# Seven block products instead of eight in some down-projection units of the first layer

## The chip, the cores and the metric

The program runs on one core of a Trainium2 chip. The metric is the device time of one execution in microseconds. A core has TensorE (PE, matmuls, with its weight loads PEld), VectorE (DVE), ScalarE (ACT), GpSimd (POOL) and SyncE (SP), which here issues the weight loads; the ACT queue issues the other DMAs. Each engine has a queue of its own and takes its instructions in order.

## The reference

A decoder trunk of two layers on 256 tokens, width 2048, all in float32: a gated-linear-attention layer, then a forgetting-attention layer, each followed by a channel mixer. What the change touches is the channel mixer:

```python
def conv_ffn(h, w_up, conv_w, conv_b, w_down):
    u = causal_dwconv(h @ w_up, conv_w, conv_b)
    a, val = split_cols(u, [FFN_HIDDEN, FFN_HIDDEN])
    return (jax.nn.silu(a) * val) @ w_down
...
        h = rmsnorm(x, norm_ffn[i])
        x = x + conv_ffn(h, ffn_w_up[i], ffn_conv_w[i], ffn_conv_b[i], ffn_w_down[i])
```

FFN_HIDDEN is 5632, so `w_down` is 5632 x 2048. The change is in the product with `w_down`, in the first layer alone.

## The kernel before

**Products.** A float32 product is made of three fast matmuls: every operand is split into a high half (rounded by a cast) and a low half (the rest), and the kernel adds high x high, low x high and high x low. Tokens are the stationary operand (blocks of 128 tokens, `b` = 0 and 1, from the lists A and B, which hold both halves of every 128-row chunk), weights are the moving one (128 x 512).

**Units and panels.** The weights lie packed in the order of use. A unit is two chunks of 128 rows by 512 columns, 128 x 1024 in SBUF. A panel is the 512 output columns of one projection over all its chunks; its two PSUM accumulators `acc` are for the two token blocks. For each unit SP loads `raw` (4 buffers), ACT casts it to `whi` (L206, 3 buffers), DVE subtracts for `wlo` (L215, 3 buffers), and PE does 2 chunks x 2 blocks x 3 = 12 matmuls: first the eight that read `whi` (L227, L228), then the four that read `wlo` (L231). `split_unit` gives the load, the cast and the subtraction a higher priority, so that they run ahead of PE as far as buffers allow.

**The channel mixer** (`ffn`) takes the hidden chunks in three parts: 16, 16 and 12. In each part the up panels come first. An up panel's output is scaled on ACT (L896), transposed on DVE (L298), written to DRAM (`turned`, L301) and read back as `u` (four reads, L306); then `taken` does the convolution (L881 on ACT, L882 and L883 on DVE), the gate (L885, L886) and the split into A (L378, L379), for two chunks. These steps are set by `later` a number of units after the panel, so those of the last up panel run while PE is in the down-projection.

**The down-projection** (`add_out`) has four panels, f = 0 to 3, of 8 units each (6 in the last part). Panels 0 and 1 go through `proj_two`: all but the last unit of panel 0, then of panel 1, then the last units; panels 2 and 3 go through `proj_tm` one after the other. At the end of a panel DVE adds the two accumulators into the residual `x` (L854). PSUM has four `acc` banks and four work banks (tags t, s, s, o).

**What sets the order.** A scheduler orders each engine's queue when the program is built, from the order and the priority in the code; `passed` counts units and starts the steps that `later` has set.

Of the kernel before, what the change touches and what calls it, by code (L numbers as in the profile page):

```python
# [135 lines left out]
def _trunk(ctx: ExitStack, tc: tile.TileContext, xt, xtok, memt, wp, wgu, gns, gfin, cnv, par, msk, out):  # L136
    nc = tc.nc
    where, _ = _layout()
    V, S, TE = nc.vector, nc.scalar, nc.tensor

    const = ctx.enter_context(tc.tile_pool(name="const", bufs=1))
    wpool = ctx.enter_context(tc.tile_pool(name="wpool", bufs=4))
# [3 lines left out]
    pacc = ctx.enter_context(tc.tile_pool(name="pacc", bufs=4, space=PSUM))  # L146
# [16 lines left out]
    x = [const.tile([P, 2, 512], F32, name=f"x{f}") for f in range(4)]  # L163
# [3 lines left out]

    with tc.high_priority(offset=2 * AHEAD):
        V.memset(bufB[KC - 1].bitcast(F32), 0.0)
# [4 lines left out]
    loads, casts, due = [], [], []  # L174

    def later(*steps):

        for units, step in steps:
            due.append([units, step])

    def passed():

        for d in due:
            d[0] -= 1
        for d in [d for d in due if d[0] == 0]:
            due.remove(d)
            with tc.issue_after(casts[-1].ins):
                d[1]()
# [3 lines left out]
    def work(tag, bufs=1):  # L192
        return pwork.tile([P, 512], F32, name="ps_" + tag, tag=tag, bufs=bufs)

    def load_unit(unit, pieces=1, before=None, pool=wpool):
        off, kcs, n = unit
        w = len(kcs) * n
        raw = wpool.tile([P, NUNIT], F32, name="raw", tag="raw", bufs=4)
        hi = pool.tile([P, NUNIT], F32R, name="whi", tag="whi", bufs=3)
        src = wp[off : off + P * w].rearrange("(p n) -> p n", p=P)  # L200
        for i in range(pieces):
            if before is not None:
                before(i)
            s = slice(i * w // pieces, (i + 1) * w // pieces)
            loads.append(nc.sync.dma_start(raw[:, s], src[:, s]))
            casts.append(S.activation(hi[:, s], raw[:, s], AF.Copy))  # L206
        return raw, hi, w

    def split_unit(unit, pieces=1, before=None, pool=wpool):
        with tc.high_priority(offset=AHEAD):  # L210
            raw, hi, w = load_unit(unit, pieces, before, pool)
            lo = pool.tile([P, NUNIT], F32R, name="wlo", tag="wlo", bufs=3)
            for i in range(pieces):
                s = slice(i * w // pieces, (i + 1) * w // pieces)
                V.tensor_tensor(lo[:, s], raw[:, s], hi[:, s].bitcast(F32), ALU.subtract)  # L215
        passed()
        return hi, lo
# [34 lines left out]
    def proj_two(keys, src, evacs, late):  # L252

        units = [where[k] for k in keys]
        base = min(min(u[1]) for u in units[0])
        acc = [[pacc.tile([P, 512], F32, name="acc", tag="acc") for _ in range(2)] for _ in keys]
        count = len(units[0])
        for part in (range(count - late), range(count - late, count)):
            for i in range(2):
                for u in part:  # L260
                    unit = units[i][u]
                    hi, lo = split_unit(unit)
                    products(list(enumerate(acc[i])), src, base, unit, hi, lo, u == 0, u == count - 1)
                if part[-1] == count - 1:
                    for b in range(2):
                        evacs[i](b, acc[i][b][:, : units[i][0][2]])

    def turned(pool, bank, width, col):

# [102 lines left out]
    def split(dst, i, src, g=None, dealt=True):  # L372

        hi, lo = dst[i][:, 0, :], dst[i][:, 1, :]
        if dealt:
            hi, lo, src = halved(hi), halved(lo), natural(src)
        if g is None:
            S.activation(hi, src, AF.Copy)  # L378
            V.tensor_tensor(lo, src, hi.bitcast(F32), ALU.subtract)  # L379
# [127 lines left out]
    with tc.tile_pool(name="load", bufs=1) as lp:  # L507
# [36 lines left out]
        sq, acc = [x[f].rearrange("p b (c t) -> p (b c) t", t=T) for f in range(2)]  # L544
# [303 lines left out]
            add_out(("wo", 1), mix, then, late=2)  # L848


    def add_out(key, src, then=None, spare=None, late=1):
        def evac(f):
            def out(b, a):
                V.tensor_tensor(x[f][:, b, :], x[f][:, b, :], a, ALU.add)  # L854
                if then is not None:
                    then(f, b)

            return out

        proj_two([(*key, f) for f in range(2)], src, [evac(f) for f in range(2)], late)  # L860
        for f in range(2, 4):
            proj_tm((*key, f), src, evac(f), spare if f == 3 else None)

    def ffn(l, nx, h, m, then, spare=None):
        with tc.tile_pool(name=f"ffn{l}", bufs=1) as fp:
            cw = fp.tile([P, 4 * 88], F32, name="cw")
            nc.sync.dma_start(cw, cnv[l])
            us = [fp.tile([P, 4, T + 2], F32, name=f"u{i}") for i in range(2)]
            for u in us:
                nc.gpsimd.memset(u[:, :, :2], 0.0)  # L870
            turn = [0]

            def taken(j, base, u, i):

                cv = []
                for c in range(2):
                    v = u[:, 2 * c + i, :]
                    col = (c * 44 + j + i) * 4
                    w = [cw[:, col + n : col + n + 1] for n in range(4)]
                    r = fp.tile([P, T], F32, name=f"cv{c}", tag=f"cv{c}", bufs=3)  # L880
                    S.activation(r, v[:, 2:], AF.Identity, bias=w[3], scale=w[2])  # L881
                    V.scalar_tensor_tensor(r, v[:, 1 : T + 1], w[1], r, ALU.mult, ALU.add)  # L882
                    V.scalar_tensor_tensor(r, v[:, :T], w[0], r, ALU.mult, ALU.add)  # L883
                    cv.append(r)
                S.activation(cv[0], cv[0], AF.Silu)  # L885
                V.tensor_tensor(cv[1], cv[0], cv[1], ALU.mult)  # L886
                split(m, j + i - base, cv[1])

            def panel(j, base, slack=0):
                held = []  # L890

                def evac(b, a):
                    if not held:
                        held.append(Turn("turned"))
                    e = tp.tile([P, 512], F32, name="scaled", tag="scaled", bufs=2)
                    S.activation(e, a, AF.Copy, scale=nx.col()[:, b : b + 1])  # L896
                    held[0].put(b, e)
                    if not b:
                        return
                    u = us[turn[0] % 2]  # L900
                    turn[0] += 1
                    later((3, held[0].write), (6, lambda: held[0].read(lambda k: u[:, k, 2:])),
                          (8 + slack, lambda: taken(j, base, u, 0)), (9 + slack, lambda: taken(j, base, u, 1)))

                return evac

            for p, (lo, hi) in enumerate(PARTS):
                js = list(range(lo, hi, 2))
                if not p:
                    proj_two([("up", l, j) for j in js[:2]], h, [panel(js[0], lo), panel(js[1], lo, 2)], 2)  # L910
                    js = js[2:]
                for j in js:
                    proj_tm(("up", l, j), h, panel(j, lo))
                end = p == len(PARTS) - 1
                add_out(("down", l, p), m, then if end else None, spare if end else None)

    def preparing(name, dst):
        n = StreamNorm()
# [147 lines left out]
```

## Time and profile before

| | |
|---|---|
| median of 3 runs | 2254.09 us (2254.07 to 2255.87) |
| profiled execution | 2254.47 us, span 2252.7 us |
| granted TensorE clock | 0.999 |
| PE busy | 2239.9 us, 10336 matmuls |
| DVE, ACT busy | 1525.7 us, 1276.5 us |
| weight loads | 427 MB on SP's queue |

Rows of the timeline read: start and length in microseconds, engine (with q: its queue issues a DMA), line, operation, tiles written <- tiles read, shapes, how many follow each other, and in brackets the idle time before and what ended it. Lines are those of the kernel before. In the profiled execution the down-projection of the first layer begins near 643.9 us (part 0), 905.1 (part 1) and 1122.6 (part 2).

### The profile page before, as it was taken

The numbers are of one execution on the slowest core, as the hardware profiler recorded it, in microseconds if no ns is written. First come the engines' busy times: TensorE is split into PE (matmuls) and PEld (weight loads), VectorE is DVE, ScalarE is ACT, GpSimd is POOL, SyncE is SP. The second block draws the span as 40 slices with busy tenths as digits, with TensorE's granted clock in tenths as the row PEclk, the third lists the DMA queues.
The fourth block names the chain that finished last, engine by engine and source line by source line (L and its number), as shares of the span: only waits on it lengthen the run. The fifth ranks groups of instructions, "written<-read, shape, count | busy, mean of one in ns | idle before, by whom it ended". The sixth has DMA issues, their size and how long they took to land.

```text
span 2252.7 us, 29275 instructions
## 1 busy us (share of the span) xinstructions
PE 2239.9 (99%) x10336; PEld 1874.8 (83%) x10336; DVE 1525.7 (68%) x2317; ACT 1276.5 (57%) x1850; POOL 2.9 (0%) x15
## 2 busy tenths in 40 slices
PE   9999999999999999999999999999999999999998
PEld 7888888888888888888888998888888888888886
DVE  7568988667675576646776556766776467664766
ACT  7555666556553565535665655555655456544654
POOL 0000000000000000000000000000000000000000
PEclk9999999999999999999999999999999999999999
DMA  9875666677775777657777876677776677766774
GB/s 318 279 233 188 207 204 220 205 233 246 250 234 195 227 237 246 209 195 247 234 250 255 257 266 202 181 251 238 244 251 216 196 240 240 242 203 210 239 242 150
DMA packets 303771, 516.96 MB, mean 229 GB/s; under 512 B 178556, under 2 KB 187272, under 8 KB 303496
## 3 DMA queue, kind: packets, MB, share of 16 engines
q1 hardware_dynamic: 124296, 427.24, 57.1%
q10 hardware_dynamic: 179328, 87.85, 13.9%
q8 instruction: 81, 1.33, 0.2%
q14 instruction: 66, 0.54, 0.1%
HBM read 470.44 MB, written 44.58 MB: 229 GB/s over the span
## 4 chain that ended last, share of the span: by engine, by line
PE 98%; DMA 1%; DVE 1%; issue 0%; ACT 0%; SPq 0%; DVEq 0%; ACTq 0%
PE acc L227 32%; PE acc L228 32%; PE acc L231 31%; DMA raw<-wp 0%; PE ps_s L683 0%; PE ps_s L485 0%; PE ps_t L478 0%; PE ps_o L496 0%; DMA xf<-xt 0%; DVE wlo L215 0%; DMA back<-turned 0%; PE ps_s L825 0%; PE ps_o L841 0%; PE ps_o L703 0%; PE ps_s L603 0%
## 5 line engine op out<-in xcount | busy, mean ns | idle before, releaser
L215 DVE TENSOR_TENSOR wlo<-raw,whi 128x1024 fp32r<-128x1024 f32 (+4 forms) x809 | 969.7, 1201 | 636.6 <-ACT whi L206 615.4
L206 ACT ACTIVATE whi<-raw 128x1024 fp32r<-128x1024 f32 (+4 forms) x809 | 842.3, 1043 | 860.0 <-PE acc L228 703.3
L227 PE MATMUL acc<-whi,B 128*128 128x512 f32 (+3 forms) x1792 | 685.7, 384 | 0.0
L228 PE MATMUL acc<-whi,B 128*128 128x512 f32 (+3 forms) x1792 | 684.5, 383 | 0.0
L227 PE MATMUL acc<-whi,A 128*128 128x512 f32 x1440 | 562.3, 392 | 1.4 <-ACT A L378 1.0
L228 PE MATMUL acc<-whi,A 128*128 128x512 f32 x1440 | 559.8, 390 | 0.0
L231 PE MATMUL acc<-wlo,B 128*128 128x512 f32 (+3 forms) x1792 | 469.3, 382 | 0.0
L231 PE MATMUL acc<-wlo,A 128*128 128x512 f32 x1440 | 387.2, 390 | 0.3 <-DVE wlo L215 0.3
L227 PEld LDWEIGHTS acc<-whi,B 128*128 128x128 f32 x1792 | 336.3, 188 | 60.5
L228 PEld LDWEIGHTS acc<-whi,B 128*128 128x128 f32 x1792 | 336.0, 188 | 59.5
L231 PEld LDWEIGHTS acc<-wlo,B 128*128 128x128 f32 x1792 | 333.7, 188 | 59.7
L227 PEld LDWEIGHTS acc<-whi,A 128*128 128x128 f32 x1440 | 270.6, 188 | 60.0 <-ACT whi L206 1.8
L228 PEld LDWEIGHTS acc<-whi,A 128*128 128x128 f32 x1440 | 270.7, 188 | 55.9 <-DVE A L382 0.2
L231 PEld LDWEIGHTS acc<-wlo,A 128*128 128x128 f32 x1440 | 270.0, 188 | 56.6 <-DVE wlo L215 0.7
L881 ACT ACTIVATE cv<-u,cw 128x256 f32<-128x256 f32 x176 | 96.9, 589 | 22.9 <-DMA u<-turned 22.9
L882 DVE SCALAR_TENSOR_TENSOR cv<-u,cw,cv 128x256 f32<-128x256 f32 x176 | 78.2, 479 | 14.9 <-ACT cv L881 14.9
L298 DVE STREAM_TRANSPOSE square<-scaled 128x512 f32<-128x512 f32 x122 | 80.0, 691 | 0.0
L883 DVE SCALAR_TENSOR_TENSOR cv<-u,cw,cv 128x256 f32<-128x256 f32 x176 | 77.1, 479 | 0.0
L854 DVE TENSOR_TENSOR x<-x,acc 128x512 f32<-128x512 f32 x64 | 41.2, 681 | 22.7 <-PE acc L231 22.7
L896 ACT ACTIVATE scaled<-acc,ny 128x512 f32<-128x512 f32 x88 | 54.8, 674 | 0.0
L462 ACT ACTIVATE sq<-x 128x256 f32<-128x256 f32 x80 | 32.5, 408 | 15.4 <-DVE x L854 14.0
L886 DVE TENSOR_TENSOR cv<-cv,cv 128x256 f32<-128x256 f32 x88 | 37.3, 424 | 1.4 <-ACT cv L885 1.4
(179 smaller groups left out, 846.3 us busy)
## 6 DMA issues: line engine op xcount, KB each, us to landing
raw<-wp SPq DMA_DIRECT2D x743, 512.0 KB, 4.2
turned<-square ACTq DMA_DIRECT2D x61, 512.0 KB, 4.5
u<-turned ACTq DMA_DIRECT2D x176, 128.0 KB, 5.2
raw<-wp SPq DMA_DIRECT2D x32, 384.0 KB, 3.1
raw<-wp SPq DMA_DIRECT2D x24, 388.0 KB, 4.5
back<-xturned ACTq DMA_DIRECT2D x64, 128.0 KB, 5.1
xturned<-square ACTq DMA_DIRECT2D x12, 512.0 KB, 4.4
back<-turned ACTq DMA_DIRECT2D x32, 128.0 KB, 4.2
```

Source lines behind the costliest of these rows:

```text
L206: casts.append(S.activation(hi[:, s], raw[:, s], AF.Copy))
L215: V.tensor_tensor(lo[:, s], raw[:, s], hi[:, s].bitcast(F32), ALU.subtract)
L227: TE.matmul(acc[:, :n], xh, hi[:, s], start=first and j == 0, stop=False)
L228: TE.matmul(acc[:, :n], xl, hi[:, s], start=False, stop=False)
L231: TE.matmul(a, xh, ls, start=False, stop=stop)
L298: V.transpose(self.square[:, :, :, b], src.rearrange("p (c t) -> p c t", t=32))
L854: V.tensor_tensor(x[f][:, b, :], x[f][:, b, :], a, ALU.add)
L881: S.activation(r, v[:, 2:], AF.Identity, bias=w[3], scale=w[2])
L882: V.scalar_tensor_tensor(r, v[:, 1 : T + 1], w[1], r, ALU.mult, ALU.add)
L883: V.scalar_tensor_tensor(r, v[:, :T], w[0], r, ALU.mult, ALU.add)
L886: V.tensor_tensor(cv[1], cv[0], cv[1], ALU.mult)
L896: S.activation(e, a, AF.Copy, scale=nx.col()[:, b : b + 1])
```

## The change

In the first layer, the units 1 and 4 of a panel pair are computed together over both panels. Such a seven unit pair is a 2 x 2 x 2 block product (two token blocks, two chunks, two panels). In place of eight block products it forms seven, by Winograd's form of Strassen's method: sums of token blocks (`forms`, made once for each part in `summed`), sums of weight blocks (`t13`, `t24`, on DVE), and sums of the products. Four of the products go to the work banks (`m1`, `m5`, `m6`, `m7`), three straight into `acc`. After the second of the two unit pairs `more` adds the work banks into `x`. `proj_seven` takes the panels of a pair unit by unit, and does so for panels 0, 1 and panels 2, 3 in parts 0 and 1, for panels 0, 1 alone in part 2: five panel pairs. The steps of one seven unit pair are: v0 (both chunks of panel 0's unit, `r0`), v2 (`t13`), v3 (`t24`), and v1 (half of panel 1's unit, `r1`), each with a cast on ACT and a subtraction on DVE, and six (v1: three) matmuls.

```diff
+SEVEN = (1, 4)
...
+    def proj_seven(keys, src, forms, evacs, pool, more):
...
+        acc = [[pacc.tile([P, 512], F32, name="acc", tag="acc") for _ in range(2)] for _ in keys]
+        m1, m5, m6, m7 = (work(t, n) for t, n in (("t", 1), ("s", 2), ("o", 1), ("s", 2)))
...
+        def emit(groups):
+            todo = [g[n] for n in range(2) for g in groups] + [g[2] for g in groups]
...
+        def halves(raw, w, name="w"):
+            hi = wpool.tile([P, NUNIT], F32R, name="whi", tag="whi", bufs=3)
+            casts.append(S.activation(hi[:, :w], raw, AF.Copy))
+            lo = wpool.tile([P, NUNIT], F32R, name="wlo", tag="wlo", bufs=3)
+            V.tensor_tensor(lo[:, :w], raw, hi[:, :w].bitcast(F32), ALU.subtract)
+            return hi, lo
...
+            if u not in forms:
+                for i in range(2):
+                    hi, lo = split_unit(units[i][u])
+                    emit([form(acc[i][b], token(kc, b), hi, lo, c) for b in range(2) for c, kc in enumerate((k0, k1))])
+                    if u == count - 1:
+                        for b in range(2):
+                            evacs[i](b, acc[i][b])
+                continue
+            s = forms[u]
+            with tc.high_priority(offset=AHEAD):
+                r0 = load(units[0][u])
+                v0 = halves(r0, NUNIT)
+                r1 = load(units[1][u])
+            passed()
+            emit([form(m1, token(k0, 0), *v0, 0), form(acc[0][0], token(k1, 0), *v0, 1)])
+            with tc.high_priority(offset=AHEAD):
+                t13 = pool.tile([P, 2, 512], F32, name="t13", tag="t13")
+                V.tensor_tensor(t13[:, 0, :], r1[:, :512], r0[:, :512], ALU.subtract)
+                V.tensor_tensor(t13[:, 1, :], r1[:, 512:], r1[:, :512], ALU.subtract)
+                v2 = halves(t13.rearrange("p c n -> p (c n)"), NUNIT)
+            emit([form(m5, s(0), *v2, 0), form(m7, s(2), *v2, 1)])
+            with tc.high_priority(offset=AHEAD):
+                t24 = pool.tile([P, 2, 512], F32, name="t24", tag="t24")
+                V.tensor_tensor(t24[:, 0, :], r1[:, 512:], t13[:, 0, :], ALU.subtract)
+                V.tensor_tensor(t24[:, 1, :], r0[:, 512:], t24[:, 0, :], ALU.subtract)
+                v3 = halves(t24.rearrange("p c n -> p (c n)"), NUNIT)
+            passed()
+            emit([form(m6, s(1), *v3, 0), form(acc[0][1], token(k1, 1), *v3, 1)])
+            with tc.high_priority(offset=AHEAD):
+                v1 = halves(r1[:, 512:], 512)
+            emit([form(acc[1][0], s(3), *v1, 0)])
+            if u == max(forms):
+                more(m1, m5, m6, m7, pool)
...
+            def more(m1, m5, m6, m7, pool):
+                u = pool.tile([P, 512], F32, name="u", tag="us", bufs=2)
+                w = pool.tile([P, 512], F32, name="w", tag="us", bufs=2)
+                V.tensor_tensor(x0[:, 0, :], x0[:, 0, :], m1, ALU.add)
+                S.activation(u, m1, AF.Copy)
+                V.tensor_tensor(u, u, m6, ALU.add)
+                V.tensor_tensor(x1[:, 0, :], x1[:, 0, :], u, ALU.add)
+                V.tensor_tensor(w, u, m7, ALU.add)
+                V.tensor_tensor(x0[:, 1, :], x0[:, 1, :], w, ALU.add)
+                V.tensor_tensor(x1[:, 1, :], x1[:, 1, :], w, ALU.add)
+                V.tensor_tensor(x1, x1, m5.unsqueeze(1).to_broadcast([P, 2, 512]), ALU.add)
...
+        if forms:
+            seven(0)
+        else:
+            proj_two([(*key, f) for f in range(2)], src, [evac(f) for f in range(2)], late)
+        if forms and then is None:
+            seven(2)
+            return
...
+            def summed(form):
+                h0, h1 = (natural(h) for h in held)
+                held.clear()
+                f = fp.tile([P, 4, P], F32, name="sf", tag="sf")
+                V.tensor_tensor(f[:, 0, :], h0[:, :, 1], h1[:, :, 1], ALU.add)
+                V.tensor_tensor(f[:, 2, :], h0[:, :, 0], h0[:, :, 1], ALU.subtract)
+                V.tensor_tensor(f[:, 1, :], f[:, 0, :], h0[:, :, 0], ALU.subtract)
+                V.tensor_tensor(f[:, 3, :], h1[:, :, 0], f[:, 1, :], ALU.subtract)
+                S.activation(form[:, 0, :, :], f, AF.Copy)
+                V.tensor_tensor(form[:, 1, :, :], f, form[:, 0, :, :].bitcast(F32), ALU.subtract)
```

The order below is of DVE's queue, with the numbers of the buffers. First the place in part 0's first panel pair where the last up panel's convolution steps stand (cv0, cv1, on u1), before:

```order
L215 TENSOR_TENSOR wlo_6197<-raw_6193,whi_6194 128x1024
L882 SCALAR_TENSOR_TENSOR cv0_6199<-u1_4577,cw_4574,cv0_6199 128x256
L882 SCALAR_TENSOR_TENSOR cv1_6203<-u1_4577,cw_4574,cv1_6203 128x256
L883 SCALAR_TENSOR_TENSOR cv0_6199<-u1_4577,cw_4574,cv0_6199 128x256
L883 SCALAR_TENSOR_TENSOR cv1_6203<-u1_4577,cw_4574,cv1_6203 128x256
L215 TENSOR_TENSOR wlo_6227<-raw_6223,whi_6224 128x1024
L882 SCALAR_TENSOR_TENSOR cv0_6229<-u1_4577,cw_4574,cv0_6229 128x256
```

Between these steps only splits of plain units stand. The same place after, from the product of the first chunk to the split of v3 (`raw_6254` is r0 and `raw_6260` r1 of unit pair 4; `wlo_6285` is v2's, `wlo_6298` v3's; L997 and L998 are the L882 and L883 of before, L1001 is L886, L466 is L379):

```order
L1001 TENSOR_TENSOR cv1_6234<-cv0_6230,cv1_6234 128x256
L338 TENSOR_TENSOR t13_6280<-raw_6260,raw_6254 128x512
L339 TENSOR_TENSOR t13_6280<-raw_6260 128x512
L997 SCALAR_TENSOR_TENSOR cv1_6266<-u1_4577,cw_4574,cv1_6266 128x256
L998 SCALAR_TENSOR_TENSOR cv0_6262<-u1_4577,cw_4574,cv0_6262 128x256
L466 TENSOR_TENSOR A14_98<-cv1_6234,A14_98 128x128x2
L344 TENSOR_TENSOR t24_6293<-raw_6260,t13_6280 128x512
L998 SCALAR_TENSOR_TENSOR cv1_6266<-u1_4577,cw_4574,cv1_6266 128x256
L310 TENSOR_TENSOR wlo_6285<-t13_6280,whi_6283 128x1024
L345 TENSOR_TENSOR t24_6293<-raw_6254,t24_6293 128x512
L953 TENSOR_TENSOR x0_80<-x0_80,ps_t_6066 128x512
L1001 TENSOR_TENSOR cv1_6266<-cv0_6262,cv1_6266 128x256
```

The sums and the splits of the second seven unit pair now stand between and behind the convolution steps, and the split of v3 (L310, `wlo_6298`) is the next row. Ahead of these rows stand, in this order, L997 on cv0 and cv1, L998 on cv0, the split of the last plain unit, L998 on cv1, v0's split and L997 on the second cv0.

The second place is the end of part 0's first panel pair, where DVE adds the accumulators into x. Before:

```order
L854 TENSOR_TENSOR x0_80<-x0_80,acc_6046 128x512
L854 TENSOR_TENSOR x0_80<-x0_80,acc_6047 128x512
L215 TENSOR_TENSOR wlo_6407<-raw_6403,whi_6404 128x1024
L854 TENSOR_TENSOR x1_81<-x1_81,acc_6048 128x512
L854 TENSOR_TENSOR x1_81<-x1_81,acc_6049 128x512
```

The two adds of a panel follow each other. After (L941 is L854; `raw_6485` and `raw_6479` belong to unit pair 1 of the next panel pair):

```order
L941 TENSOR_TENSOR x0_80<-x0_80,acc_6062 128x512
L338 TENSOR_TENSOR t13_6493<-raw_6485,raw_6479 128x512
L339 TENSOR_TENSOR t13_6493<-raw_6485 128x512
L216 TENSOR_TENSOR wlo_6465<-raw_6461,whi_6462 128x1024
L941 TENSOR_TENSOR x0_80<-x0_80,acc_6063 128x512
```

Two sums and a split now stand between the adds of panel 0. The third place is the end of part 2's first panel pair, after:

```order
L216 TENSOR_TENSOR wlo_10311<-raw_10307,whi_10308 128x1024
L941 TENSOR_TENSOR x0_80<-x0_80,acc_9973 128x512
L958 TENSOR_TENSOR x0_80<-x0_80,w_10232 128x512
L959 TENSOR_TENSOR x1_81<-x1_81,w_10232 128x512
L216 TENSOR_TENSOR wlo_10329<-raw_10325,whi_10326 128x1024
L385 STREAM_TRANSPOSE square_10264<-x0_80 128x512
L941 TENSOR_TENSOR x0_80<-x0_80,acc_9974 128x512
```

Here two adds of `more`, a split and a transpose stand between the two adds of panel 0.

More of the change, by code (lines that the diff above doesn't have):

```diff
@@ L848, in fox, with add_out @@
             add_out(("wo", 1), mix, then, late=2)
-    def add_out(key, src, then=None, spare=None, late=1):
+    def add_out(key, src, then=None, spare=None, late=1, forms=None, pool=None):
         def evac(f):
@@ L858, in evac, with seven @@
             return out
[L860 removed]
+        def seven(f):
+            x0, x1 = x[f], x[f + 1]
+            def more(m1, m5, m6, m7, pool):
[9 more added lines that the diff above has]
+                V.tensor_tensor(x1, x1, m5.unsqueeze(1).to_broadcast([P, 2, 512]), ALU.add)
+            proj_seven([(*key, g) for g in (f, f + 1)], src, forms, [evac(f), evac(f + 1)], pool, more)
+        if forms:
[5 more added lines that the diff above has]
+            return
         for f in range(2, 4):
@@ L871, in ffn, with form @@
             turn = [0]
+            forms = {u: fp.tile([P, 2, 4, P], F32R, name=f"forms{u}") for u in (SEVEN if spare is None else ())}
+            held = []
+            def form(t):
+                return lambda i: [t[:, h, i, :] for h in range(2)]
             def taken(j, base, u, i):
@@ L914, in ffn @@
                 end = p == len(PARTS) - 1
-                add_out(("down", l, p), m, then if end else None, spare if end else None)
+                add_out(("down", l, p), m, then if end else None, spare if end else None,
+                        forms={u: form(t) for u, t in forms.items()}, pool=fp)
     def preparing(name, dst):
```

36 lines of the change are left out of this document (added).

## The prediction

> **What bounds the kernel now.** I read the page first, for the engines and the chain that ended last.
>
> ```profile
> span 2252.7 us, 29275 instructions
> PE 2239.9 (99%) x10336; PEld 1874.8 (83%) x10336; DVE 1525.7 (68%) x2317; ACT 1276.5 (57%) x1850; POOL 2.9 (0%) x15
> PE 98%; DMA 1%; DVE 1%; issue 0%; ACT 0%; SPq 0%; DVEq 0%; ACTq 0%
> ```
>
> TensorE (PE) is busy 99% of the span and is 98% of the chain. So a matmul that goes is time won, and whatever makes PE wait is time lost, since no later slack takes it back. The change removes matmuls and adds VectorE (DVE) work, so I next read the busy time by stage: both panel pairs of part 0, the first pairs of parts 1 and 2.
>
> ```profile
> 643.90:687.40 43.50, 43.50 (x193) 36.05 (x192) 27.31 (x35) 22.30 (x28) 0.00 (x0) 1.00 0.68 218
> 687.40:730.90 43.50, 43.50 (x193) 36.04 (x192) 21.98 (x21) 16.96 (x17) 0.00 (x0) 1.00 0.57 195
> 905.00:948.50 43.50, 43.50 (x193) 36.04 (x192) 27.31 (x35) 22.31 (x28) 0.00 (x0) 1.00 0.68 218
> 1122.60:1155.30 32.70, 32.70 (x146) 27.07 (x145) 23.01 (x33) 19.68 (x32) 0.31 (x1) 1.00 0.71 230
> ```
>
> The columns are the stretch, then PE, PEld, DVE, ACT and POOL busy (instructions), the granted clock and DMA. PE never pauses; DVE has 27.3 of 43.5 us in a first pair of 16 chunks, 22.0 in a second, 23.0 of 32.7 in part 2: a first pair still holds the convolution of the last up panels. The timeline of PE gives the rhythm, and the waits of part 0's down stage say what ACT and DVE wait for.
>
> ```profile
> 643.90 0.39 PE L227 MATMUL acc<-whi,A 128*128 128x512 f32 x1
> 644.13 0.39 PE L228 MATMUL acc<-whi,A 128*128 128x512 f32 x1
> 645.72 1.07 PE L231 MATMUL acc<-wlo,A 128*128 128x512 f32 x4
> 646.62 0.39 PE L227 MATMUL acc<-whi,A 128*128 128x512 f32 x1
> ACT whi L206 <- PE acc L228: 45.4, 28, 3.0
> DVE wlo L215 <- ACT whi L206: 34.7, 25, 2.3
> ```
>
> A unit of 12 matmuls takes 2.72 us, so 0.227 a matmul. ACT waits only for PE to give a whi buffer back, DVE for ACT: today both run as far ahead as three buffers let them.
>
> **What goes.** Eight block products of three matmuls become seven: 3 x 0.227 = 0.68 us for each seven unit pair. Five panel pairs with two such pairs each make 30 matmuls, **-6.8 us**. The number of loads is the same.
>
> **What is added, and whether it is hidden.** Prices are start to start where rows follow each other:
>
> ```profile
> 37.27 0.69 DVE L550 TENSOR_TENSOR x<-x 128x512 f32<-128x512 f32 x1
> 37.87 3.49 DVE L215 TENSOR_TENSOR wlo<-raw,whi 128x1024 fp32r<-128x1024 f32 x3
> 645.49 1.30 DVE L298 STREAM_TRANSPOSE square<-scaled 128x512 f32<-128x512 f32 x2
> 646.71 0.61 DVE L379 TENSOR_TENSOR A<-cv,A 128x256 fp32r<-128x256 f32 x1
> 659.03 0.87 DVE L882 SCALAR_TENSOR_TENSOR cv<-u,cw,cv 128x256 f32<-128x256 f32 x2
> 659.83 0.87 DVE L883 SCALAR_TENSOR_TENSOR cv<-u,cw,cv 128x256 f32<-128x256 f32 x2
> 660.62 1.22 DVE L215 TENSOR_TENSOR wlo<-raw,whi 128x1024 fp32r<-128x1024 f32 x1
> 661.75 0.87 DVE L882 SCALAR_TENSOR_TENSOR cv<-u,cw,cv 128x256 f32<-128x256 f32 x2
> 662.55 0.42 DVE L886 TENSOR_TENSOR cv<-cv,cv 128x256 f32<-128x256 f32 x1
> 662.88 0.88 DVE L883 SCALAR_TENSOR_TENSOR cv<-u,cw,cv 128x256 f32<-128x256 f32 x2
> 664.81 0.63 DVE L379 TENSOR_TENSOR A<-cv,A 128x256 fp32r<-128x256 f32 x1
> 665.27 0.43 DVE L886 TENSOR_TENSOR cv<-cv,cv 128x256 f32<-128x256 f32 x1
> ```
>
> So 0.60 for 512 columns (37.27 to 37.87), 1.14 for 1024, 0.40 for a convolution step, 0.33 for its product, 0.61 for a transpose, 0.46 for the low half of A. A seven unit pair adds four sums of 512 (2.4) and splits 3.5 x 1024 instead of 2 (1.7): DVE has 2.3 + 4.1 = 6.4 us of work where PE now needs 21 x 0.227 = 4.76. Two of them and the eight-step end sum, whose seven DVE steps cost 6 x 0.60 + 1.14 = 4.7, add 12.9 us to a panel pair: 40.2 of 42.1 us in the first pairs of parts 0 and 1, 34.9 in their second pairs, and 35.9 in part 2's first pair, which has 31.3. On average that fits in four of the five pairs. The question is the place, because DVE takes its instructions in order. I count d from the first down matmul (643.90 is d = 0). Without waits PE would be in the first seven pair from d = 5.44 to 10.20 and in the second from 21.08 to 25.84, with 1.36 for each of the forms v0, v2, v3 and 0.68 for v1; each needs its wlo 0.91 (v1: 0.45) after it begins.
>
> *First seven pair.* Its sums need the second unit's load, which goes out when an earlier raw is split (the row below, 636.13 + 1.23) and lands 4.2 later, near 641.6, d = -2.3.
>
> ```profile
> 636.13 1.23 DVE L215 TENSOR_TENSOR wlo<-raw,whi 128x1024 fp32r<-128x1024 f32 x1 [1.49 <-ACT whi L206]
> raw<-wp SPq DMA_DIRECT2D x743, 512.0 KB, 4.2
> ```
>
> From there DVE's queue up to the split of v3 holds four sums of 512 (2.4), three splits (3.4), two convolution steps and two products (1.5), two low halves (0.9), two transposes (1.2) and v3's split (1.22): 10.6, so d = 8.3. PE wants it at 9.07. It fits by 0.7, so 0; up to 0.7 lost if the load is late, and a gain is excluded, as PE does not wait there today.
>
> *Second seven pair.* Its sums stand in DVE's queue behind the convolution steps of the last up panel, and these hang on a DMA chain: transposes, turned out, u back, ACT, DVE.
>
> ```profile
> 646.82 0.34 ACTq L301 DMA_DIRECT2D turned<-square  x1
> 651.92 2.17 ACTq L306 DMA_DIRECT2D u<-turned  x4
> 656.80 1.06 ACT L206 ACTIVATE whi<-raw 128x1024 fp32r<-128x1024 f32 x1 [1.53 <-PE acc L228]
> 657.76 1.08 ACT L881 ACTIVATE cv<-u,cw 128x256 f32<-128x256 f32 x2
> DMA to landing us min/median/max: 3.9/4.5/5.6
> ```
>
> Before, turned goes out at 646.82 (d = 2.9) and the third of the four reads is there by about 657.8. After, the two transposes stand behind the first pair's sums and splits and end near d = 5.6, so turned goes out 2.7 later; with 5.1 to the first read, 1.0 to the third and the median 4.5 to its landing (the last row, for these reads), ACT's convolution step follows at d = 16.3 and DVE's, L997 on cv1, at 17.0. DVE is in order, and from this step on its queue holds it and three more convolution steps, the splits of the last plain unit and of v0, a product, t13 (1.2), two steps, a low half, a t24 step, one more step and the split of v2: 7 x 0.40 + 2 x 1.14 + 0.33 + 1.2 + 0.46 + 0.60 + 1.22 = 8.9, so d = 25.9, where PE wanted it at 23.35. Then the second t24 step ends at 26.5, ACT's cast of v3 takes 1.06 (row 656.80) and DVE's split 1.22: d = 28.9 against 24.71. PE loses **4.2 us** here. Bounds: with 5.6 for the reads and a slow turned the step begins at 18.5, 5.7 lost; it can't begin before about 15.4 (before, the pair that begins at 659.03 has its second at 15.5), 2.6 lost. Part 1 is the same. In part 2 the order is kinder before v2 (24.3) and worse behind it, since a low half, an add and a product stand ahead of the t24 step: v3 at 28.8, 4.1 lost.
>
> *Ends of pairs.* The next pair needs the old accumulators read out.
>
> ```profile
> 684.45 1.28 DVE L854 TENSOR_TENSOR x<-x,acc 128x512 f32<-128x512 f32 x2 [0.85 <-PE acc L231]
> 685.65 1.22 DVE L215 TENSOR_TENSOR wlo<-raw,whi 128x1024 fp32r<-128x1024 f32 x1
> 687.17 1.28 DVE L854 TENSOR_TENSOR x<-x,acc 128x512 f32<-128x512 f32 x2 [0.30 <-PE acc L231]
> ```
>
> Before, both adds of a panel follow each other 3 us before its bank is wanted. After, between the two of panel 0 stand two sums and a split: 0.60 + 1.2 + 1.14 + 0.68 = 3.6 from 2.95 before the next pair begins (684.45 to 687.40), so 0.65 behind its start, and the bank is wanted at 0.45: 0.2 lost (0 to 0.9 with a late load), in parts 0 and 1. In part 2 only one unit pair lies between the second seven pair and the end, and the end sum is queued there. From v3's split on, DVE holds v1's split (0.60), four splits (4.56), six adds of 512 (3.6), a transpose (0.61) and the second add (0.68) = 10.05, PE until it wants the bank 0.45 + 0.68 + 5.44 + 0.45 = 7.02: **3.0 lost** (2.3 to 3.7).
>
> *No cost:* `summed` in the up panels (PE does not wait there and DVE idles about 1.4 of each 2.72 us) and the casts on ACT (22 of 43 us busy).
>
> **The sum.** -6.8 + 2 x (4.2 + 0.2) + 4.1 + 3.0 = +9.1 us. The profiled execution took 2254.47 us, 0.4 above the median of 2254.09; on the median, **2263.2**. With all low bounds (2.6 in each part, 0 and 2.3 at the ends) it is +3.3, 2257.4; with all high ones (5.7, 0.9, 3.7, and 0.7 in each first seven pair) +17.9, 2272.
>
> **Rivals.**
> *Hidden after all (faster):* the three buffers carry DVE through, only the 30 matmuls count: 2254.1 - 6.8 = 2247.3. For it: DVE idles 34.7 us before the splits of part 0's down stage. It decides if DVE begins L997 on cv1 in the second seven pairs by d = 12.8, 4.2 ahead of the forecast. Against it: before, it begins there at 15.5, and from v0 on the same three buffers hold 1.36 us each instead of 2.72.
> *Half hidden (same):* the reads land as early as ACT can take them and DVE's steps overlap more; 1.5 to 2.5 lost in each second seven pair, 1.5 at part 2's end: about 2254.1 - 6.8 + 6 + 1.7 = 2255.0. It decides if DVE begins L997 on cv1 before d = 15.
>
> *Waits that cool PE (still slower):* the first eight matmuls of the run, after 1.45 us of idle, take 3.92 us instead of 1.81.
>
> ```profile
> 1.45 3.78 PE L172 MATMUL ps_o<-B 128*128 128x512 f32 x8 [1.45 <-DVE B L169]
> 5.37 1.22 PE L227 MATMUL acc<-whi,A 128*128 128x512 f32 x2
> ```
>
> If each of the four long waits brought such a start again, 4 x 2.1 = 8.4 more: 2271.6. No wait forecast as one piece is over 3.0 us. The Trainium skill, "TensorE: Matmul & The Clock Gate", section "HAM oscillation", states that idle gaps over about 3.4 us halve the clock; by it the forecast stands unless two waits run together. The granted clock of the page reads full already in that first stretch, so the trace cannot confirm it.
>
> **How the numbers follow.** Forecast 0.70, hidden 0.10, half hidden 0.13, cooled 0.07. The forecast's own range is 2257.4 to 2272; I reach down to 2256 for part of the half-hidden case, leave the hidden one out, and stop at 2271, since not all bounds are high at once. About 0.2% (4.5 us) is what a measurement of this kernel can tell from no change. Faster 0.10, same 0.14, slower 0.76.
>
> **What would show it.** Right: PE idle before matmuls that read wlo or whi, with DVE or ACT as releaser, about 4 us in the second seven pair of each part's first panel pair, next to none in the second panel pairs, and 3 us before part 2's third panel, released by DVE's add of x0. PE waits for DVE and ACT of about 16 us in all, and 10306 matmuls. Wrong: no PE wait in these places, or waits in the first seven pairs, or matmuls that are slower without a wait.

## The result and the profile after

The changed kernel takes 2278.05 us (median of 4 runs, 2276.8 to 2278.55) beside 2254.98 for the kernel before: a ratio of 1.0101 (95% interval 1.0084 to 1.0119). It is slower, as forecast, but by 23 us where 9 were forecast, and above the upper end of the range, 2271. The profiled execution took 2278.55 us.

The page after, with the span, the busy times and the chain that ended last:

```profile
span 2276.8 us, 29418 instructions
PE 2245.8 (99%) x10306; PEld 1869.9 (82%) x10306; DVE 1597.1 (70%) x2442; ACT 1297.9 (57%) x1881; POOL 2.9 (0%) x15
PE 91%; DMA 4%; DVE 3%; issue 1%; ACT 1%; ACTq 0%; SPq 0%; DVEq 0%
```

The 30 matmuls are gone, yet PE is busy for 5.9 us more, and the chain now holds DMA and DVE. The windows of the three down stages (to the first matmul of the next stage) say where; the columns are those of the prediction's windows, the first three rows are of before, the last three of after:

```profile
643.90:730.95 87.05, 87.05 (x386) 72.10 (x385) 49.35 (x55) 39.31 (x44) 0.00 (x0) 1.00 0.62 206
905.02:992.06 87.04, 87.04 (x385) 72.10 (x384) 49.34 (x55) 39.31 (x44) 0.00 (x0) 1.00 0.63 206
1122.62:1187.90 65.28, 65.28 (x289) 54.07 (x288) 46.94 (x62) 39.57 (x68) 0.31 (x1) 1.00 0.80 255
```

```profile
643.46:737.00 93.54, 89.20 (x373) 70.85 (x372) 74.98 (x93) 47.12 (x56) 0.00 (x0) 0.96 0.59 191
911.08:1005.75 94.67, 89.02 (x374) 71.09 (x372) 74.84 (x93) 47.23 (x56) 0.00 (x0) 0.96 0.58 189
1136.31:1209.93 73.62, 67.37 (x284) 52.80 (x282) 61.22 (x87) 44.50 (x75) 0.31 (x1) 0.98 0.69 213
```

The stages grow by 6.5, 7.6 and 8.3 us, 22.5 together. Of the other 1.6 between the spans, 2.1 are a wait in the forgetting-attention layer, which the change does not touch and in which other runs wait too, 0.3 to 1.5 us, and -0.4 lies at the start. The clock column falls below 1 in all three. PE's waits in part 0, from its timeline:

```profile
664.68 0.50 PE L290 MATMUL ps_t<-whi,A 128*128 128x512 f32 x1 [0.81 <-ACT whi L308]
670.43 1.84 PE L290 MATMUL ps_s<-whi,forms 128*128 128x512 f32 x4 [2.37 <-ACT whi L308]
672.63 1.22 PE L290 MATMUL ps_s<-wlo,forms 128*128 128x512 f32 x2 [0.36 <-DVE wlo L310]
674.40 0.80 PE L290 MATMUL ps_o<-whi,forms 128*128 128x512 f32 x1 [0.55 <-ACT whi L308]
675.42 0.63 PE L290 MATMUL ps_o<-whi,forms 128*128 128x512 f32 x1
```

All lie in the second seven unit pair of the first panel pair; the first seven pair and the second panel pairs have none. Matmuls that wait for nothing also stretch: rows that follow each other stood 0.227 apart before, and from 675.00 to 675.42 to 675.85 it is 0.42. The clock by stretches of 6 and 7 us:

```profile
664.00:670.00 6.00, 3.13 (x10) 1.64 (x10) 6.00 (x12) 3.26 (x6) 0.00 (x0) 1.00 0.29 87
670.00:677.00 7.00, 5.66 (x12) 3.58 (x13) 6.73 (x10) 4.40 (x8) 0.00 (x0) 0.55 0.24 75
```

The trace has the granted clock at 0.5 from 670.74 to 677.56, from 940.39 to 947.22 and from 1162.26 to 1165.67, and nowhere in the kernel before until its matmuls are over (2246.7). Splitting each start-to-start time into 0.227, a stretch under the low clock and the rest gives, for the three parts: waits in the second seven pair 6.3, 7.4 and 6.0; stretch 2.5, 2.7 and 1.2; elsewhere in the stage 0.4, 0.3 and 2.5. These 29.3 less 6.8 for the matmuls make the 22.5.

### The profile page after: what moved, and what is told of

Read it like the earlier page. It is cut to its first block, busy times and chain, and to the rows that moved or that the text cites. A ratio compares the mean times of both kernels' runs of the same rounds, so it can differ in the third digit from the quotient of the medians.

```text
span 2276.8 us, 29418 instructions
## 1 busy us (share of the span) xinstructions
PE 2245.8 (99%) x10306; PEld 1869.9 (82%) x10306; DVE 1597.1 (70%) x2442; ACT 1297.9 (57%) x1881; POOL 2.9 (0%) x15
## 4 chain that ended last, share of the span: by engine, by line
PE 91%; DMA 4%; DVE 3%; issue 1%; ACT 1%; ACTq 0%; SPq 0%; DVEq 0%
PE acc L228 27%; PE acc L229 27%; PE acc L232 27%; PE acc L290 5%; DMA raw<-wp 1%; DMA u<-turned 1%; DMA turned<-square 1%; DMA xturned<-square 1%; DVE wlo L216 1%; PE ps_s L770 0%; DMA back<-xturned 0%; ACT whi L207 0%; PE ps_s L572 0%; PE ps_o L290 0%; PE ps_t L565 0%
## 5 line engine op out<-in xcount | busy, mean ns | idle before, releaser
L216 DVE TENSOR_TENSOR wlo<-raw,whi 128x1024 fp32r<-128x1024 f32 (+4 forms) x789 | 943.5, 1200 | 562.8 <-ACT whi L207 533.6
L207 ACT ACTIVATE whi<-raw 128x1024 fp32r<-128x1024 f32 (+4 forms) x789 | 819.9, 1042 | 797.4 <-PE acc L229 588.0
L228 PE MATMUL acc<-whi,A 128*128 128x512 f32 x1136 | 443.9, 393 | 3.3 <-ACT whi L207 2.1
L229 PE MATMUL acc<-whi,A 128*128 128x512 f32 x1136 | 441.5, 390 | 0.0
L232 PE MATMUL acc<-wlo,A 128*128 128x512 f32 x1136 | 305.9, 390 | 0.5 <-DVE wlo L216 0.5
L228 PEld LDWEIGHTS acc<-whi,A 128*128 128x128 f32 x1136 | 213.0, 188 | 51.0 <-ACT whi L207 4.5
L232 PEld LDWEIGHTS acc<-wlo,A 128*128 128x128 f32 x1136 | 212.8, 188 | 45.5 <-DVE wlo L216 1.4
L229 PEld LDWEIGHTS acc<-whi,A 128*128 128x128 f32 x1136 | 213.3, 188 | 44.3 <-DVE A L469 0.4
L290 PE MATMUL acc<-whi,A 128*128 128x512 f32 x488 | 128.7, 393 | 0.0
L290 PEld LDWEIGHTS acc<-whi,A 128*128 128x128 f32 x488 | 92.7, 190 | 19.6
L997 DVE SCALAR_TENSOR_TENSOR cv<-u,cw,cv 128x256 f32<-128x256 f32 x176 | 78.8, 479 | 29.9 <-ACT cv L996 29.7
L998 DVE SCALAR_TENSOR_TENSOR cv<-u,cw,cv 128x256 f32<-128x256 f32 x176 | 77.4, 478 | 0.0
L290 PE MATMUL acc<-wlo,A 128*128 128x512 f32 x244 | 69.4, 392 | 0.3
L941 DVE TENSOR_TENSOR x<-x,acc 128x512 f32<-128x512 f32 x64 | 41.5, 681 | 20.2 <-PE acc L232 15.1
```

The costliest lines, as they stand in the source:

```text
L228: TE.matmul(acc[:, :n], xh, hi[:, s], start=first and j == 0, stop=False)
L229: TE.matmul(acc[:, :n], xl, hi[:, s], start=False, stop=False)
L232: TE.matmul(a, xh, ls, start=False, stop=stop)
L290: TE.matmul(a, x, w, start=k not in begun, stop=calls[k] == 0)
```

## Experiments

**Which seven pairs cost.** Four kernels take other units; each is the changed kernel with a table for `SEVEN`, by part and first panel of the pair:

```diff
-SEVEN = (1, 4)
+SEVEN = {(0, 2): (1, 4), (1, 2): (1, 4)}                            # second_pairs
+SEVEN = {k: (1,) for k in ((0,0), (0,2), (1,0), (1,2), (2,0))}      # unit1_alone
+SEVEN = {(0, 0): (4,), (1, 0): (4,), (2, 0): (4,)}                  # unit4_alone
+SEVEN = {(0,0): (1,6), (0,2): (1,6), (1,0): (1,6), (1,2): (1,6), (2,0): (1,)}   # units_1_and_6
```

*Second panel pairs alone:*

> Seven unit pairs (units 1 and 4) only in panels 2 and 3 of parts 0 and 1, where no convolution of an up panel runs beside them; all first pairs as before the change. 12 matmuls fewer, 2.7 us. Theory (the loss comes from the second seven pair of a first panel pair, where DVE waits for the last up panel's reads, and from the clock that falls behind it): no PE wait there, 2254.9 - 2.7 = 2252.2. Rival (any seven pair costs, since DVE has 6.4 us of work in 4.8): each of the four loses at least its 0.68 again, 2255 or more.

Measured: 2253.54 against 2255.09, ratio 0.9993 (0.9983 to 1.0002). Part 0's stage is 87.2 us, part 1's 86.0: of 1.36 us of matmuls saved in each, 1.5 and 0.3 come back, mostly as waits (the longest 0.6). Part 0 thus fits the rival and part 1 the theory; but of the 23 us hardly any are there.

*Unit 1 alone, in all five pairs:*

> Only unit 1 is a seven pair, in all five panel pairs; 15 matmuls fewer, 3.4 us. Theory: the first seven pairs did not make PE wait in the changed kernel; the reads of u come later but nothing that PE needs stands behind them, 2251.5 with full clock throughout. Rival (the late transposes and the burst of loads behind the first seven pair alone hold up DVE and ACT for several us): PE waits of 2 us or more in the units behind it, 2255 to 2262.

Measured: 2257.26 (2254.2 to 2261.2), ratio 1.0010 (1.0000 to 1.0019), full clock. No wait in the seven pairs; 0.6 and 1.6 us at the ends of the first panel pairs of parts 0 and 1, where PE waits for DVE's sums into x, and 1.1 in part 2, where it waits for ACT's half of A, which comes behind the convolution. The reads of u are already late: medians 6.6, 6.2 and 6.1 us.

*Unit 4 alone, in the three first pairs:*

> Only unit 4 of the three first panel pairs is a seven pair; 9 matmuls fewer, 2.0 us. The transposes of the last up panel then leave DVE as early as before the change. Theory (reads of u that land late because of the first seven pair make up a good part of the loss): the reads land in 4 to 5 us, PE loses 2 to 3 us in each of the three places and the clock stays full: 2254.9 - 2.0 + 8 = 2261. Rival (the order of DVE's queue in the second seven pair alone makes the loss): 6.5 to 8.5 us in each as in the changed kernel, 2275.

Measured: 2257.24, ratio 1.0009 (0.9999 to 1.0019). This was the surprise, below both forecasts: the same second seven pair costs 0.1 us in parts 0 and 1 (both stages 0.58 shorter for 0.68 saved); only part 2 loses 4.1, in several waits of at most 1.0. With no first seven pair ahead of them the reads go out at 650.3 and land in time. The reads of u in part 0, from the groups by line (first after, then this kernel; the landing row is microseconds from issue to landing):

```profile
L393 ACTq DMA_DIRECT2D u<-turned x4: 366/472/648, 654.2 to 655.7; - x4
DMA to landing us min/median/max: 6.8/7.7/7.9
```

```profile
L393 ACTq DMA_DIRECT2D u<-turned x4: 367/528/548, 650.3 to 651.8; - x4
DMA to landing us min/median/max: 2.8/2.9/4.6
```

So the second pair is dear mostly because the first one stands ahead of the transposes: it delays the reads, and what then goes out beside them might slow them, which a later run tests. One thing more differs here: DVE's queue has the second pair's t13 ahead of the convolution steps, so this run alone does not part the two.

*Units 1 and 6, away from the convolution steps:*

> In parts 0 and 1 the second seven pair is unit 6 instead of unit 4, behind the convolution of the last up panel; part 2 has unit 1 alone. 27 matmuls fewer, 6.1 us. Theory: the seven pair away from the convolution steps costs nothing, full clock, 2254.9 - 6.1 = 2248.8; perhaps 1 us lost at the ends of the pairs, where the end sum now stands. Rival (DVE's total work of a first pair, 40 of 42 us, is the bound): waits move to unit 6 and the time stays near 2270.

Measured: 2261.97, ratio 1.0034 (1.0024 to 1.0043), full clock; 13 us above the theory and 8 below the rival. The waits moved to the ends of the pairs, which I had put at 1 us: with unit 6 the end sum into x stands ahead of the reading out of the accumulators.

```profile
PE acc L290 <- DVE x L941: 3.7, 2, 1.9
PE acc L228 <- DVE x L941: 1.9, 2, 1.0
```

**DVE's queue apart from the reads.** The order of every engine stays; the convolution of each part's last up panel reads the other u buffer, which is there already (so part of the output is computed from other numbers):

```diff
-                          (8 + slack, lambda: taken(j, base, u, 0)), ...
+                          (8 + slack, lambda: taken(j, base, used, 0)), ...    # used: the other u for the last panel
```

> The changed kernel with one difference: the convolution of each part's last up panel reads the buffer of the panel before, which landed long ago, so that its steps don't wait for the reads of u (which still go out); that part of the output is not the reference's. Every engine's queue is in the same order. Theory (late reads hold DVE's in-order queue): the waits of 6.7 to 8.5 us in each second seven pair and the half clock go in parts 0 and 1; part 2 keeps about 2 at its end. 2278 - 6.7 - 2.5 - 7.7 - 2.7 - 7 = about 2252. Rival (DVE's own work and the order of its queue, read from its durations alone, cost 2.6 each and more): 2258 to 2262. Rival (the reads don't matter): 2278.

Measured: 2262.26, ratio 1.0037 (1.0023 to 1.0051); full clock. This is the upper edge of the first rival's range, and 10 us above the theory. The reads are about as slow as in the changed kernel (8.8, 7.0 and 6.6 us), but nothing on PE's path hangs on them. Waits of 2.5, 2.6 and 3.3 us are left in the second seven pairs. The windows of its stages:

```profile
643.51:731.29 87.78, 85.74 (x373) 69.53 (x372) 74.75 (x93) 46.91 (x56) 0.00 (x0) 1.00 0.64 203
905.37:993.07 87.70, 85.62 (x373) 69.61 (x372) 75.04 (x94) 47.47 (x56) 0.00 (x0) 1.00 0.64 204
1123.63:1193.22 69.59, 65.65 (x284) 52.42 (x282) 60.47 (x85) 43.76 (x75) 0.31 (x1) 1.00 0.70 225
```

They are 5.8, 7.0 and 4.0 us shorter than after's, 16.8 together, and 5.7 longer than before's. So even without waiting for the reads the change is slower, by 5.7 us in these stages (7.5 by the medians); waiting for the reads, with the low clock that comes with it, makes the rest.

**Are the reads slow because weight loads are bunched beside them?** In the timeline of after, SP sends loads of 512 KB at 652.63, 654.09, 655.23 and 657.07 around the four reads (654.2 to 655.7), where before one went out every 2.72 us. The test puts more loads beside the reads in the kernel *before*, with no seven block products:

```diff
             loads.append(nc.sync.dma_start(raw[:, s], src[:, s]))
+            if len(loads) in (234, 330, 410):
+                for spare_raw in extra:          # two or four buffers that nobody reads
+                    nc.sync.dma_start(spare_raw, src)
```

> The kernel before, with the same order on PE, DVE and ACT; SP issues, in each part's first down panel pair, two more copies of one weight load (2 x 512 KB, into spare buffers that nobody reads) right behind the load that goes out 0.4 to 1.0 us ahead of the four reads of u (651.03, 912.2 and 1129.8 in the kernel before). No sums, no seven block products. Theory A (the reads land late in the changed kernel because weight loads are bunched beside them): 1.05 MB more at the 280 GB/s seen there take 3.7 us, so the reads' median landing grows from 4.5, 3.5 and 5.4 us to 6.5 to 9 us in each part, with VectorE's work unchanged. Theory B (they are late for another reason, such as the later write of turned or the place in ACT's queue): the medians stay within 1 us of 4.5, 3.5 and 5.4. Time: 2254 to 2258 by A, 2254 to 2255 by B.

> The same with four more copies (2.1 MB, 7.5 us at 280 GB/s). Theory A: the reads' medians go on growing, to 8 to 13 us, at least 1.5 us above the run with two copies. Theory B: within 1 us of 4.5, 3.5 and 5.4 again. If the medians grow with two copies and not with four, the number of loads is not what sets them.

Measured: 2259.12 and 2265.91 (one run each; before 2256.57). The copies had nothing to wait for, and the scheduler put all of them near 422 to 434 us, so the reads of the down stages tell nothing (medians 4.1 and 4.8 in part 0). What they gave is a note on the clock, below. The same with the copies bound behind their load:

```diff
-                for spare_raw in extra:
-                    nc.sync.dma_start(spare_raw, src)
+                with tc.issue_after(loads[-1].ins):
+                    for spare_raw in extra:
+                        nc.sync.dma_start(spare_raw, src)
```

> The kernel before with two more copies of a weight load per part (2 x 512 KB, buffers that nobody reads), this time bound to go out right behind the load of 651.03, 912.2 and 1129.8, which is 0.4 to 0.9 us ahead of the four reads of u; in the two earlier runs the scheduler had sent all copies near 422 to 434 us, so that they told nothing of the reads. PE's order is that of the kernel before; one convolution step and one copy on DVE and ACT change places behind the reads. Theory A (bunched weight loads make the reads land late): the medians grow from 4.5, 3.5 and 5.4 us to 6.5 to 9 us. Theory B (another reason): within 1 us of 4.5, 3.5 and 5.4. Time: up to 6 us above the kernel before by A, as the convolution steps come later, 1 us by B.

> The same with four copies (2.1 MB, 7.5 us at 280 GB/s). Theory A: medians of 8 to 13 us, at least 1.5 us above the run with two. Theory B: within 1 us of 4.5, 3.5 and 5.4. PE's wait in the earlier run with four copies was 5.5 us in one piece and the granted clock went to 0.5 for 6.8 us 3.5 us after it; waits of under 2 us in one piece should leave it at 1.

Measured (one run each, before 2256.57): 2257.49 and 2259.49. The clock's time named in the last text is wrong: it was low from 445.46 to 452.29, beginning within the wait that ended at 447.91. The reads and the stage of part 0 with two copies:

```profile
L310 ACTq DMA_DIRECT2D u<-turned x4: 394/524/4489, 652.5 to 654.0; - x4
DMA to landing us min/median/max: 9.7/9.9/10.0
644.54:731.58 87.04, 87.04 (x386) 72.07 (x384) 49.76 (x56) 39.07 (x44) 0.00 (x0) 1.00 0.69 218
```

The medians go from 4.5, 3.5 and 5.4 to 9.9, 9.5 and 8.6 us with two copies, and to 10.5, 10.5 and 10.3 with four. So loads sent just ahead are enough to make the reads land late, as theory A has it; the second dose adds 0.6 to 1.7, less than it asked in two of the three parts. That the bunch is what delays them in the changed kernel is not shown as directly: the copies go out closer together, and with them ACT spends up to 4.5 us on issuing a single read (5.1 with four), in the changed kernel 0.9 at most. It fits a kernel that comes below, units 2 and 5: there the reads go out about as late (653.3), but between loads at 651.84 and 657.24, and land in 3.1 us.

A second reading is worth as much. With two copies the reads take 3 to 6 us longer and cost the kernel before nothing (part 0's stage still takes 87.04 us, and PE waits in none of the three). With four the stages grow by 2.0, 1.1 and 0.8 us: there a cast of weights, which PE needs, has come to stand behind the convolution steps in ACT's queue. Late reads are dear where something that PE needs stands behind the steps that wait for them, as DVE's sums do in the changed kernel.

**The clock.** The changed kernel, with 18 matmuls on a zero operand put ahead of v0 (4), v2 (10) and v3 (4) in the second seven pairs of the first panel pairs. They add nothing to the accumulator, only work for PE while it would wait:

```diff
+        def keep_warm(n):
+            if first and u == max(forms):
+                for _ in range(n):
+                    TE.matmul(acc[0][0], nought, src[0], start=False, stop=False)
...
+            keep_warm(10)
             emit([form(m5, s(0), *v2, 0), form(m7, s(2), *v2, 1)])
```

> The changed kernel with 18 matmuls more in each second seven pair of a first panel pair (weights of zeros, added to an accumulator): 3 or 4 ahead of v0, 10 ahead of v2, 4 ahead of v2's low ones, 4.1 us of work placed where PE waited 6.7 to 8.5 us. Theory A (the half clock costs about 2.5 + 2.7 + 1.2 = 6.4 us by itself): the clock stays full, 2271.7. Theory B (DVE's chain sets the end there and the half clock runs beside its waits): the clock stays full and the time falls by 2 us at most, 2276 to 2278. If the extra matmuls cost time, it is over 2278.

Measured: 2275.17 (2272.0 to 2276.1), ratio 1.0088 (1.0073 to 1.0103), between the two theories. The granted clock is full in all three stages. Part 0's stretch, and a wait behind it (L951 is after's L941):

```profile
664.00:670.00 6.00, 5.72 (x26) 4.49 (x25) 6.00 (x12) 2.72 (x5) 0.00 (x0) 1.00 0.29 87
670.00:677.00 7.00, 5.84 (x24) 3.94 (x23) 6.63 (x10) 4.96 (x7) 0.00 (x0) 1.00 0.39 125
693.10 1.15 PE L297 MATMUL acc<-whi,A 128*128 128x512 f32 x4 [0.84 <-DVE x L951]
```

Its stages are 1.1, 1.1 and 2.1 us shorter than after's, but this is not the price of the low clock alone. Up to the end of the second seven pair PE has lost 6.8, 7.7 and 6.8 us (the 4.1 of zeros included) against after's 8.8, 10.1 and 7.2: 2.0, 2.4 and 0.4 less. Of these 0.95 and 0.7 in parts 0 and 1 come from reads that happened to land earlier (DVE's step on cv1 begins 19.3 and 20.2 us into the stage, after's at 20.3 and 20.9); in part 2 it begins 0.2 later. What is left, about 1.0, 1.7 and 0.6, is an estimate of the low clock's net price: some 3 us, not the 6.4 of stretched matmuls, since part of the stretch ran while DVE's chain was what PE waited for in any case. Behind these pairs the stages differ for other reasons: the filled kernel loses 1.1 and 1.3 us more to DVE's adds into x (the last row), and in part 2 2.0 less to a late cast, of which more below.

**A version that gains.** The first attempt keeps the transposes ahead of any seven pair, with units 2 and 5 in the four pairs of parts 0 and 1; the second takes unit 4 alone in the first pairs, units 2 and 5 in the second; part 2 stays as before in both:

```diff
+SEVEN = {(0, 0): (2, 5), (0, 2): (2, 5), (1, 0): (2, 5), (1, 2): (2, 5)}    # units_2_and_5
+SEVEN = {(0, 0): (4,), (0, 2): (2, 5), (1, 0): (4,), (1, 2): (2, 5)}        # unit4_then_2_and_5
```

> Units 2 and 5 instead of 1 and 4 in all four panel pairs of parts 0 and 1, part 2 as before the change; 24 matmuls fewer, 5.4 us. The first seven pair begins 5.4 us later, so the transposes of the last up panel leave DVE before its sums. Theory (reads are late because the transposes stand behind the sums and because the released buffers send four loads in a bunch beside them): the reads land in 3 to 5 us, no half clock, at most 2 us lost at the ends of pairs: 2250 to 2252. Rival (two seven pairs overload DVE wherever they stand in a first panel pair): waits of 4 us or more in each first pair, 2258 or more.

> Candidate for a faster version: unit 4 alone in the first panel pairs of parts 0 and 1 (which cost PE 0.1 us of waits where it was tried), units 2 and 5 in the second pairs, part 2 as before the change; 18 matmuls fewer, 4.1 us. Theory: 2255.0 - 4.1 + 1 = 2252. Rival (ends of the pairs lose what is won): 2254 to 2256.

Measured: 2251.82, ratio 0.9985 (0.9976 to 0.9994), and 2251.03, ratio 0.9984 (0.9975 to 0.9994), against 2254.72. They beat the kernel before by 2.9 and 3.7 us, as their theories had it; this is a little less than the 0.2% named above, but both intervals lie under 1, which no other version's does. The windows of the last one's two stages:

```profile
643.57:728.92 85.35, 85.35 (x377) 70.40 (x375) 69.00 (x86) 45.20 (x52) 0.00 (x0) 1.00 0.64 204
903.00:988.35 85.35, 85.35 (x376) 70.40 (x375) 68.64 (x85) 45.20 (x52) 0.00 (x0) 1.00 0.64 204
```

Each saves 1.70 of the 2.04 us that its nine matmuls took: DVE works 69 us there instead of 49, and PE hardly notices.

## Why the prediction was right in direction and wrong in size

**What goes: right.** 10306 matmuls, and 0.227 each.

**First seven pair: right.** PE waits nowhere in it, in any part. The prediction did not follow its other effect: by delaying the transposes it moved the reads beside a bunch of loads, two of which (SP at 654.09 and 655.23) are the second seven pair's own.

**Second seven pair: the step that failed.** The chain of steps was as told: turned out late, reads, ACT's step, DVE's step on cv1, the queue behind it. The first read was forecast at d = 10.7 and went out at 10.8 (654.23, with d = 0 at 643.46). Then the term "the median 4.5 to its landing" met 7.7, 8.6 and 7.1 us. I had taken it from the kernel before, as if the reads' company would stay. From the timelines of DVE and ACT of after:

```profile
663.08 0.60 ACT L996 ACTIVATE cv<-u,cw 128x256 f32<-128x256 f32 x1 [2.77 <-DMA u<-turned]
663.72 0.48 DVE L997 SCALAR_TENSOR_TENSOR cv<-u,cw,cv 128x256 f32<-128x256 f32 x1 [2.89 <-ACT cv L996]
671.35 1.23 DVE L310 TENSOR_TENSOR wlo<-t,whi 128x1024 fp32r<-128x1024 f32 x1
673.29 1.06 ACT L308 ACTIVATE whi<-t 128x1024 fp32r<-128x1024 f32 x1 [2.60 <-DVE t L345]
674.38 1.23 DVE L310 TENSOR_TENSOR wlo<-t,whi 128x1024 fp32r<-128x1024 f32 x1 [0.27 <-ACT whi L308]
```

DVE's step on cv1 begins at d = 20.3 instead of 17.0, 3.3 late (20.9 and 20.3 in parts 1 and 2). The queue behind it was as long as forecast: the split of v2 ends at 29.1 instead of 25.9, that of v3 at 32.1 instead of 28.9. With 20.3 in its place the prediction's own working gives 7.5 us lost in part 0; the trace has 6.3 of waits and 2.5 of stretch, of which about 1.0 is the low clock's net price by the estimate above. In parts 1 and 2 the waits are 7.4 and 6.0, against 4.2 and 4.1. The high bound, 5.7, was too low, since its 5.6 for the reads was the slowest read of a stage in which nothing was bunched. The low bound, 2.6, is what the kernel that does not await the reads showed: 2.5 and 2.6 in parts 0 and 1, with the step on cv1 at 15.2 and 15.6, where the bound had put it (15.4).

**Ends of pairs.** Parts 0 and 1: 0.2 forecast, 0.4 and 0.3 measured for the whole rest of the stage. None of it is a wait for DVE's adds, so this match is partly luck; in the filled kernel, where the load for the sums came late, they cost 1.1 and 1.3, above the bound's 0.9. Part 2: 3.0 forecast, 0.2 measured. I had the second bank wanted at once; but in that panel PE runs through one token block first and comes to the other only later, so only the first add of x0 was in its way. What cost 2.3 us there was something else: ACT's queue waited for the reads that feed the next layer (`back`), and the cast of weights that PE needs stood behind them (PE's row first, then ACT's):

```profile
1198.24 0.50 PE L228 MATMUL acc<-whi,A 128*128 128x512 f32 x1 [1.35 <-ACT whi L207]
1197.13 1.06 ACT L207 ACTIVATE whi<-raw 128x1024 fp32r<-128x1024 f32 x1 [4.69 <-DMA back<-xturned]
```

**The rivals.** Both hidden cases are out: DVE's step came at 20.3, neither by 12.8 nor before 15. "Waits that cool PE" got 0.07 and came true in three places. I set it aside since no wait was over 3.0 us in one piece, and the Trainium skill, "TensorE: Matmul & The Clock Gate", section "HAM oscillation", speaks of gaps over about 3.4 us. The traces disagree with that as a threshold for one wait: the clock fell after 2.37, 2.37 and 2.43 us. The price I put on it, 8.4, was too high (some 3 us net by the filled kernel).

**The sum.** Forecast lost in the three stages: 8.4 + 4.1 in the second seven pairs and 0.4 + 3.0 at the ends, 15.9. Measured: 19.7 and 3.2, and 6.4 of stretch under the low clock that was not in the sum, 29.3. The 13.4 between them, with the 2.1 in the next layer and -0.4 at the start, are the 15 us by which the profiled execution exceeds its forecast. What was counted was counted rightly but for the reads and part 2's end; what was left out is what the change does to the company of the reads and to the clock.

## What to carry to other kernels

When extra work delays the step that starts a DMA, the DMA's old latency no longer holds: look at which other transfers will then go out beside it, and at what stands behind it in the in-order queues. Put such work where the DMA is already out, as the last version does: the same kind of edit, with 18 matmuls fewer instead of 30, then gains 3.7 us instead of losing 23. In a kernel in which PE is 99% busy, several waits close together can cost more than their sum, since the clock can go down with them (some 3 of the 23 us here).

## What the runs showed of the hardware that I had not expected

*The clock.* It fell to 0.5 for 6.83, 6.83 and 3.41 us. PE's waits before, in us: 0.8 and 2.4; 1.5, 2.4 and half of one of 1.0, during which it fell; 0.3 and 2.4; and in the run with four early copies 5.5 in one piece, where it fell during the wait:

```profile
447.91 0.80 PE L230 MATMUL acc<-whi,A 128*128 128x512 f32 x1 [5.46 <-ACT whi L209]
445.40:452.20 6.80, 4.29 (x10) 3.42 (x11) 1.23 (x1) 1.06 (x1) 0.00 (x0) 0.50 1.10 362
```

But it stayed full after 2.43 us in the kernel that does not await the reads, and after 0.7 and 2.6 us (443 to 449) with two early copies. So neither a single length nor the idle time within the last 3.4 us (2.2 to 3.0 us ahead of a fall, up to 2.6 without one) divides the cases here; where the line runs stays open.

*Small reads beside large loads.* Four reads of 128 KB land after 2.9 us (median) with little beside them and after 10 with 1 MB more of loads sent just ahead; two further copies add only 0.6 to 1.7.
